# Four instead of three seven-product pairs in six value/gate panels of a retention layer, two in a row, and one factor moved from VectorE to ScalarE

## Chip, core and metric

One core of one Trainium2 chip runs the whole program. The metric is device time in microseconds (us) of that core. The kernel before takes 2566.95 us (median of three runs, 2566.91 to 2567.36).

## The reference

Two decoder layers over 256 positions of width 2048, in float32: a retention layer and a block-sparse attention layer, each followed by a gated MLP. Only the retention layer's input projection is touched here. Cut to that:

```
proj = h @ w_in                       # 256x2048 @ 2048x12288
q, k, v, g = split(proj)              # per head: q, k 256 wide; v, g 512 wide
inner = (q @ k.T) * decay             # chunked retention, 8 heads
o = inner @ v                         # (plus the state between chunks)
on = (o - mean(o)) * rsqrt(var(o) + eps)
y = silu(g) * on * gain               # then y @ w_out
```

## The kernel before

**Products in three parts.** Each float32 weight is used as a high part `wh` and a low part `wl` that add up to it, and so is each activation. A product takes three matmuls: high by high, high by low, low by high. ScalarE makes `wh` by a copy (line 221), and VectorE makes `wl` by a subtraction from the raw weight and `wh` (line 222). The weights stream from HBM into four buffers `raw` (1 MB each); `wh` and `wl` have four buffers each of 128x1024.

**Steps.** The program is one long list of steps, and each step consumes one buffer of `wh` and one of `wl`. `step` (through `issue_split`) emits the splits for the step three ahead, then the matmuls of the present one. Since there are four buffers, the split for a step can only be written when the matmuls of the step four before it are done. Tile's scheduler fixes the order of each engine's instructions when the program is built; each engine then runs its own list in that order, and semaphores order the engines against one another.

**A head.** Each of the eight retention heads (hd = 0 to 7 here; "two to seven" of the change are hd = 1 to 6) has three panels: q and k (four steps each, lines 344 and 347), then value and gate together (`panel_s`, line 390). The value/gate panel walks over the 2048 rows of the contraction in eight pairs of 128-row chunks. A pair is done in one of two ways.

- **Eight** (`A` in the sequence): two steps of 12 matmuls, eight products in all. It needs two splits of 128x1024.
- **Seven** (`S`): Winograd's form of Strassen's scheme, seven products, 21 matmuls, in four steps. Call them s1 (products 1 and 3, 6 matmuls), s2 (product 2, 3 matmuls), s3 (products 5 and 7, 6) and s4 (products 4 and 6, 6). The weights have to be combined first, in place in `raw`: after the split for s1, one 128x1024 addition (line 237) makes the blocks that s3 takes, and two 128x512 additions (lines 242 and 243) make those that s4 takes. s1, s3 and s4 have a 128x1024 split each, s2 one of 128x512. The activations' combinations ("forms") are made once, when `fresh` is set (line 410 on), and kept in four slots that lie in the not yet written end of `yT`.

`HEAD_SEQS` gives the order. Before: `AASASASA` with pairs 0, 2 and 4 as sevens in heads 0 to 6, and `AASAASAA` with two sevens in the last head. Between a head's second and third pair also come its scores (`ret_scores`: 12 small matmuls into `ps`, then on VectorE the product with the decay `pf`, on ScalarE its high part `ph`, on VectorE the low part `pl`).

**The end of a head.** In the next head's q panel, `ret_pv` multiplies by the values, takes mean and variance, has GpSimd compute the factor `rs` = (var + eps)^-0.5 (line 578), subtracts the mean and multiplies by silu(g) into `sg` (line 845), and multiplies `sg` by `rs` (line 847). Two steps later `ret_yT` transposes `sg` on TensorE (line 540) into `yT`.

Of the kernel before, what the change touches and what calls it, by code (L numbers as in the profile page):

```python
# [13 lines left out]
AF = mybir.ActivationFunctionType  # L14
ALU = mybir.AluOpType
# [4 lines left out]
S = 256  # L20
KC = D // P
RH, RDK, RDV = 8, 256, 512
# [46 lines left out]
def wide_seqs(first, second, n_slots=8):  # L69


    n = len(second)
    one = [(p, first.index(p) % n_slots if p in first else None, p in first) for p in range(n)]
    again = [(i % n_slots, p, False) for i, p in enumerate(first)][-n_slots:]
    again += [(again[i][0], p, True) for i, p in enumerate(first[:-n_slots])]
    again = again[: second.count("S")]
    others = [p for p in range(n) if p not in [q for _, q, _ in again]]
    two = []
    for c in second:
        slot, p, fresh = again.pop(0) if c == "S" else (None, others.pop(0), False)  # L80
        two.append((p, slot, fresh))
    return one, two


def head_seq(pairs, seq, fresh):

    again, others = list(enumerate(pairs)), [p for p in range(len(seq)) if p not in pairs]
    return [(*again.pop(0)[::-1], fresh) if c == "S" else (others.pop(0), None, False) for c in seq]


FFN_SEVENS = list(range(3, 22, 2))
FFN_SEQS = wide_seqs(FFN_SEVENS, "AAASASASASASASASASASAA")
RET_SEQS = wide_seqs([5, 7, 9, 11, 13, 15], "AAASASASASASAAAA")
HEAD_SEQS = [head_seq([0, 2, 4], "AASASASA", hd == 0) for hd in range(RH - 1)] + [head_seq([0, 2], "AASAASAA", False)]
MOB_SEQS = wide_seqs([3, 5, 7], "AAASAAAA")


def build(tc, a, out):
# [11 lines left out]
    act, dve, pe = nc.scalar, nc.vector, nc.tensor  # L110
# [171 lines left out]
    def emit(items):  # L282
        for unit, mms in items:
            units.append(unit)
            for hf, mm in enumerate(mms):
                emit_half(len(units) - 1, *(mm if isinstance(mm, tuple) else (hf, mm)))
# [225 lines left out]
    def aux_tile():  # L512

        if not wide[0]:
            return paux.tile([P, 512], F32, name="aux")
        if not spare:
            t = pacc.tile([P, 2, 512], F32, name="acc")
            spare.extend([t[:, 1, :], t[:, 0, :]])
        return spare.pop()

    def mm3(dst, lh, ll, rh, rl, start, stop):
        pe.matmul(dst, lhsT=lh, rhs=rh, start=start, stop=False)  # L522
        pe.matmul(dst, lhsT=lh, rhs=rl, start=False, stop=False)  # L523
        pe.matmul(dst, lhsT=ll, rhs=rh, start=False, stop=stop)  # L524
# [50 lines left out]
    def rstd(dst, src, mul, eps):  # L575
        v = sml.tile([P, 2], F32, name="v")
        dve.tensor_scalar(v, src, mul, eps, op0=ALU.mult, op1=ALU.add)
        nc.gpsimd.tensor_tensor(dst, v, mhalf, op=ALU.pow)
# [87 lines left out]
    def make_temps(pool, **tags):  # L666

        return lambda what: pool().tile([P, 512], F32, name=what, tag=tags[what])
# [96 lines left out]
    def ret_vg(then):  # L765

        m, sums, came = {}, {}, []

        def first():
            a, b = (ret["p1"].tile([P, 2, RDV], F32, name=n, tag=t) for n, t in (("sa", "qT"), ("sb", "kT")))  # L770
            sums.update({2: a[:, 0, :], 4: a[:, 1, :], 3: b[:, 0, :], 8: b[:, 1, :]})
            act.activation(sums[2], m[1], AF.Copy)
            dve.tensor_tensor(sums[3], m[6], sums[2], op=ALU.subtract)
            dve.tensor_tensor(sums[4], m[7], sums[3], op=ALU.add)

        def second():
            dve.tensor_tensor(sums[3], m[5], sums[3], op=ALU.add)
            dve.tensor_tensor(sums[8], m[5], sums[4], op=ALU.add)

        def tiles():  # L780
            ret["v"] = [ret["p1"].tile([P, 2, RDV], F32R, name=n) for n in ("vh", "vl")]
            ret["sg"] = ret["p1"].tile([P, 2, RDV], F32, name="sg")

        def done(b, acc):
            m[b] = acc
            if b == 6:
                after(0, first)
                after(1, second)
            if b not in (2, 3, 4, 8):
                return  # L790
            if not came:
                tiles()
            came.append(b)
            t, v = int(b in (4, 8)), sums[b]
            rt = r["r"][:, t : t + 1]
            dve.tensor_tensor(v, acc, v, op=ALU.subtract if b == 4 else ALU.add)
            if b in (3, 8):
                act.activation(ret["sg"][:, t, :], v, AF.Silu, scale=rt)
            else:
                vh, vl = (x[:, t, :] for x in ret["v"])  # L800
                act.activation(vh, v, AF.Copy, scale=rt)
                dve.scalar_tensor_tensor(vl, v, rt, vh.bitcast(F32), op0=ALU.mult, op1=ALU.subtract)
            if len(came) == 4:
                then()
        return done
# [20 lines left out]
    def ret_pv(hd):  # L826

        ph, pl = ret.pop(("p", hd))
        vh, vl = ret["v"]
        sg = ret["sg"]  # L830
        mv = sml.tile([P, 2, 2], F32, name="mv")
        po = [None, None]
        for t in range(2):
            po[t] = aux_tile()
            blocks = [(0, 0)] if t == 0 else [(P, 0), (S, 1)]
            for i, (c0, m) in enumerate(blocks):
                mm3(po[t], ph[:, c0 : c0 + P], pl[:, c0 : c0 + P], vh[:, m, :], vl[:, m, :],
                    i == 0, i == len(blocks) - 1)
            st = sml.tile([P, 6], F32, name="st")
            dve.bn_stats(st, po[t])  # L840
            dve.bn_aggr(mv[:, t, :], st)
        rs = sml.tile([P, 2], F32, name="rs")
        rstd(rs, mv[:, :, 1], 1.0, GN_EPS)
        for t in range(2):
            dve.scalar_tensor_tensor(sg[:, t, :], po[t], mv[:, t, 0:1], sg[:, t, :],
                                     op0=ALU.subtract, op1=ALU.mult)
            dve.tensor_scalar(sg[:, t, :], sg[:, t, :], rs[:, t : t + 1], None, op0=ALU.mult)

    def ret_yT(hd):
        y = ret["sg"]  # L850
# [11 lines left out]
    def ret_head(hd):  # L862
        def k_done(acc):
            ret_qk("k")(acc)
            after(4, lambda: ret_scores(hd))

        def vg_done():
            after(3, lambda: ret_pv(hd))
            after(5, lambda: ret_yT(hd))
            if hd == 0:  # L870
                after(6, lambda: bias_load())
                after(8, lambda: bias_table())

        q = panel_b(w_in, hd * RDK, xT_h, ret_qk("q"), before=ret_begin if hd == 0 else None)
        k = panel_b(w_in, D + hd * RDK, xT_h, k_done)
        if hd == 0:
            emit_pairs(q, k)
        else:
            emit(q + k)

        def unit(k0):
            vg = w_in[k0 * P : (k0 + 2) * P, 2 * D :].rearrange("(c p) (b n) -> p c b n", p=P, b=2)
            return vg[:, :, :, hd * RDV : (hd + 1) * RDV], 1024

        def slots(s):

            c = (28, 30, 24, 26)[s]
            return yT[0][:, c, :], yT[0][:, c + 1, :]

        emit(panel_s(unit, xT_h, HEAD_SEQS[hd], make_temps(lambda: ret["p1"], af="bs", ff="m1"), ret_vg(vg_done), slots))  # L890

# [296 lines left out]
```

## Time and profile before

| | before |
|---|---|
| median of three runs | 2566.95 us |
| profiled execution | 2566.55 us |
| its span, first to last instruction | 2564.8 us |
| TensorE (PE) busy | 2551.7 us, 99% |
| VectorE (DVE) busy | 2096.4 us, 82% |
| ScalarE (ACT) busy | 1445.2 us, 56% |
| mean granted TensorE clock | 0.999 of 2.4 GHz |
| bytes moved | 504.94 MB, mean 197 GB/s |

The 1.75 us between execution and span lie outside the instructions. Busy times of TensorE are sums of pipelined matmuls that overlap, so the pace of the matmuls is read from the distance of their starts, not from their durations. One retention head lasts 68.1 us.

### The profile page before, as it was taken

To read this page: it belongs to the slowest core of one execution; us is meant where nothing else is said; L and a number is where in the kernel's file an instruction comes from. 1 tells how busy PE (TensorE), PEld (TensorE's weight loads), DVE (VectorE), ACT (ScalarE), POOL (GpSimd) and SP (SyncE) were. 2 spreads that over 40 slices of the span, in tenths; PEclk is the share of its full clock that TensorE was granted. 3 is DMA by queue.
4 is the path that set the end of the run, shared out by engine and by line. 5 is a ranking of instruction groups with operands and counts; after the bars stand their busy time and mean duration, and the time that the engine had idled before them with its cause. 6 is when DMAs were issued, how large, how long until landed. Compare 5 with 4: busy or idle time off the path is not lost.

```text
span 2564.8 us, 34472 instructions
## 1 busy us (share of the span) xinstructions
PE 2551.7 (99%) x13280; PEld 2175.4 (85%) x13280; DVE 2096.4 (82%) x2740; ACT 1445.2 (56%) x1866; POOL 10.2 (0%) x24
## 2 busy tenths in 40 slices
PE   9999999999999999999999999999999999999998
PEld 8888888888888888888888888888888888888887
DVE  7888888898877777777898866668877777778998
ACT  6555555555555555555565655455655555555655
POOL 0000000000000000000000000000000000000000
PEclk9999999999999999999999999999999999999999
DMA  7765665555566566656665665555665656567654
GB/s 258 227 203 181 197 193 185 181 185 192 197 197 193 193 198 193 198 192 199 228 213 201 209 193 177 174 183 170 193 195 191 199 188 203 188 203 240 214 202 148
DMA packets 344532, 504.94 MB, mean 197 GB/s; under 512 B 9632, under 2 KB 260528, under 8 KB 344112
## 3 DMA queue, kind: packets, MB, share of 16 engines
q1 hardware_dynamic: 332720, 483.53, 57.5%
q10 hardware_dynamic: 11648, 19.22, 2.2%
q8 instruction: 104, 1.70, 0.3%
q14 instruction: 60, 0.49, 0.1%
HBM read 495.34 MB, written 10.51 MB: 197 GB/s over the span
## 4 chain that ended last, share of the span: by engine, by line
PE 97%; DVE 2%; ACT 1%; issue 0%; POOL 0%; POOLq 0%; ACTq 0%; DVEq 0%
PE acc L344 35%; PE aux L390 31%; PE acc L347 17%; PE acc L390 8%; PE acc L310 1%; PE acc L312 1%; PE acc L311 1%; DVE wl L222 1%; PE aux L540 1%; PE aux L523 0%; PE aux L524 0%; PE aux L522 0%; ACT wh L221 0%; PE aux L1110 0%; PE acc L523 0%
## 5 line engine op out<-in xcount | busy, mean ns | idle before, releaser
L221 ACT ACTIVATE wh<-raw 128x1024 fp32r<-128x1024 f32 (+2 forms) x1065 | 1083.8, 1028 | 1013.9 <-PE acc L344 459.0
L222 DVE TENSOR_TENSOR wl<-raw,wh 128x1024 fp32r<-128x1024 f32 (+2 forms) x1065 | 1240.9, 1182 | 407.6 <-ACT wh L221 398.9
L344 PE MATMUL acc<-hT,wh 128*128 128x512 f32 x3840 | 1208.9, 396 | 1.2 <-DVE hT L546 0.8
L347 PEld LDWEIGHTS acc<-hT,wl 128*128 128x128 f32 x3840 | 721.0, 188 | 170.3 <-DVE wl L222 0.6
L347 PE MATMUL acc<-hT,wl 128*128 128x256 f32 x3840 | 755.2, 278 | 0.2 <-DVE wl L222 0.2
L344 PEld LDWEIGHTS acc<-hT,wh 128*128 128x128 f32 x3840 | 586.2, 189 | 4.0 <-ACT wh L221 1.6
L390 PE MATMUL aux<-wh,actT 128*128 128x512 f32 x952 | 312.3, 389 | 0.0
L390 PE MATMUL aux<-wh,hT 128*128 128x512 f32 x854 | 285.1, 390 | 0.4 <-ACT wh L221 0.2
L390 PEld LDWEIGHTS aux<-wh,actT 128*128 128x128 f32 x952 | 178.7, 188 | 37.7 <-DVE h L620 0.5
L390 PEld LDWEIGHTS aux<-wh,hT 128*128 128x128 f32 x854 | 160.2, 188 | 35.1 <-ACT wh L221 1.6
L390 PE MATMUL aux<-wl,actT 128*128 128x512 f32 x476 | 185.2, 389 | 0.0
L390 PE MATMUL aux<-wl,hT 128*128 128x512 f32 x427 | 166.3, 390 | 0.0
L929 DVE SCALAR_TENSOR_TENSOR t<-u,cw,t 128x256 f32<-128x256 f32 x352 | 146.6, 478 | 0.0
L390 PE MATMUL aux<-wh,yT 128*128 128x512 f32 x426 | 141.8, 391 | 0.5 <-ACT yT L221 0.5
L390 PE MATMUL acc<-wh,hT 128*128 128x512 f32 x364 | 133.5, 390 | 0.0
L390 PEld LDWEIGHTS aux<-wl,actT 128*128 128x128 f32 x476 | 89.4, 188 | 18.2
L925 ACT ACTIVATE t<-u,cw 128x256 f32<-128x256 f32 x176 | 95.0, 586 | 0.1
L390 PEld LDWEIGHTS aux<-wh,yT 128*128 128x128 f32 x426 | 80.0, 188 | 17.6 <-ACT yT L221 0.9
L390 PEld LDWEIGHTS aux<-wl,hT 128*128 128x128 f32 x427 | 80.2, 188 | 16.7 <-DVE wl L222 0.3
L237 DVE TENSOR_TENSOR raw<-raw 128x1024 f32<-128x1024 f32 x76 | 92.5, 1217 | 0.0
L390 PE MATMUL aux<-wl,yT 128*128 128x512 f32 x213 | 83.0, 390 | 0.0
L745 DVE TENSOR_TENSOR bs<-acc,bs 128x512 f32<-128x512 f32 x120 | 81.9, 683 | 0.0
(208 smaller groups left out, 2024.2 us busy)
## 6 DMA issues: line engine op xcount, KB each, us to landing
raw<-in_ffn_w_up_dram SPq DMA_DIRECT2D x176, 1024.0 KB, 5.2
raw<-in_ffn_w_down_dram SPq DMA_DIRECT2D x88, 1024.0 KB, 5.5
raw<-in_ret_w_in_dram SPq DMA_DIRECT2D x133, 512.0 KB, 4.8
raw<-in_moba_w_qkv_dram SPq DMA_DIRECT2D x48, 1024.0 KB, 5.3
raw<-in_ret_w_out_dram SPq DMA_DIRECT2D x32, 1024.0 KB, 5.4
raw<-in_ret_w_in_dram SPq DMA_DIRECT2D x29, 1024.0 KB, 5.7
raw<-in_moba_w_out_dram SPq DMA_DIRECT2D x16, 1024.0 KB, 5.4
hT<-f ACTq DMA_DIRECT2D x22, 256.0 KB, 5.4
```

The source lines that it names most:

```text
L221: in_turn(act.activation(hi, src, AF.Copy))
L222: in_turn(dve.tensor_tensor(lo, src, hi.bitcast(F32), op=ALU.subtract))
L237: dve.tensor_tensor(b[:, 0:2, :], b[:, 0:4:3, :], b[:, 1:2, :].to_broadcast([P, 2, 512]), op=ALU.add)
L310: pe.matmul(acc, lhsT=xh, rhs=wh[:, c, :], start=(k == 0), stop=False)
L311: pe.matmul(acc, lhsT=xh, rhs=wl[:, c, :], start=False, stop=False)
L312: pe.matmul(acc, lhsT=xl, rhs=wh[:, c, :], start=False, stop=(k == nk - 1))
L344: pe.matmul(acc[:, b, :], lhsT=wh[:, c, b * P : (b + 1) * P], rhs=xt[:, k, :], start=(k == 0), stop=False)
L347: pe.matmul(acc[:, b, S:], lhsT=wl[:, c, b * P : (b + 1) * P], rhs=xt[:, k, :S], start=False, stop=(k == KC - 1))
L390: pe.matmul(acc[b], lhsT=xs, rhs=ws, start=(n == 1), stop=(n == uses[b]))
L745: dve.tensor_tensor(bs, acc[:, :, :S], bs, op=ALU.add)
L925: act.activation(t[:, i, :], u[:, i, 2:], AF.Identity, bias=c[:, 3, b : b + 1], scale=c[:, 2, b : b + 1])
L929: dve.scalar_tensor_tensor(t[:, i, :], u[:, i, tap : tap + S], c[:, tap, b : b + 1], t[:, i, :], op0=ALU.mult, op1=ALU.add)
```

## The change

Three things. In heads 1 to 6 the panel has four sevens, pairs 0, 2, 4 and 6, in the order `AASSASSA`: each time two sevens stand next to each other. Head 1 makes the forms for the new pair 6; heads 2 to 6 reuse them. Heads 0 and 7 keep their sequences. And in all eight heads the multiplication of `sg` by `rs` is an activation on ScalarE with a scale.

```
 def head_seq(pairs, seq, fresh):
-    again, others = list(enumerate(pairs)), [p for p in range(len(seq)) if p not in pairs]
-    return [(*again.pop(0)[::-1], fresh) if c == "S" else (others.pop(0), None, False) for c in seq]
+    again = [(p, i, p in fresh) for i, p in enumerate(pairs)]
+    others = [p for p in range(len(seq)) if p not in pairs]
+    return [again.pop(0) if c == "S" else (others.pop(0), None, False) for c in seq]
...
-HEAD_SEQS = [head_seq([0, 2, 4], "AASASASA", hd == 0) for hd in range(RH - 1)] + [head_seq([0, 2], "AASAASAA", False)]
+HEAD_SEQS = [head_seq([0, 2, 4], "AASASASA", [0, 2, 4])] + [head_seq([0, 2, 4, 6], "AASSASSA", [6] if hd == 1 else []) for hd in range(1, RH - 1)]
+HEAD_SEQS += [head_seq([0, 2], "AASAASAA", [])]
...
-            dve.tensor_scalar(sg[:, t, :], sg[:, t, :], rs[:, t : t + 1], None, op0=ALU.mult)
+            act.activation(sg[:, t, :], sg[:, t, :], AF.Copy, scale=rs[:, t : t + 1])
```

The change shifts all later lines by two: L222 of before is L224 of the changed kernel, L237 is L239, L820 is L822.

VectorE's list in the value/gate panel of head 4 (heads 2 to 6 have the same), from the scores to the third seven. `wl` 128x1024 and 128x512 are the splits, `raw` the additions, `pf` and `pl` the scores. Before:

```order
L222 TENSOR_TENSOR wl<-raw,wh 128x1024 x2
L820 TENSOR_TENSOR pf<-acc,dec 128x256
L821 TENSOR_TENSOR pf<-acc,dec 128x128
L823 TENSOR_TENSOR pl<-pf,ph 128x384
L222 TENSOR_TENSOR wl<-raw,wh 128x1024 x3
L222 TENSOR_TENSOR wl<-raw,wh 128x512
L237 TENSOR_TENSOR raw<-raw 128x1024
L242 TENSOR_TENSOR raw<-raw 128x512
L243 TENSOR_TENSOR raw<-raw 128x512
L222 TENSOR_TENSOR wl<-raw,wh 128x1024 x5
```

And the changed kernel, same place:

```order
L224 TENSOR_TENSOR wl<-raw,wh 128x1024 x2
L822 TENSOR_TENSOR pf<-acc,dec 128x256
L823 TENSOR_TENSOR pf<-acc,dec 128x128
L825 TENSOR_TENSOR pl<-pf,ph 128x384
L224 TENSOR_TENSOR wl<-raw,wh 128x1024
L224 TENSOR_TENSOR wl<-raw,wh 128x512
L239 TENSOR_TENSOR raw<-raw 128x1024
L244 TENSOR_TENSOR raw<-raw 128x512
L245 TENSOR_TENSOR raw<-raw 128x512
L224 TENSOR_TENSOR wl<-raw,wh 128x1024 x5
```

In both, the first row holds the splits of s3 and s4 of the first seven. Before, the next three 128x1024 splits are the two of an eight and s1 of the next seven; now the very next split is s1 of the second seven, and its additions follow with no eight between. The row of five is then s3, s4, the two of an eight, and s1 of the third seven; the fourth seven follows the third in the same way.

VectorE's list in head 1, where the forms are made, in the changed kernel: `af` and `ff` are the forms, `yT` 128x512 is the low part that goes into the slot. Before, the rows of `ff` and `yT` are absent, and in the second seven the addition of line 243 (L245 here) precedes the split of s3; the rest stands in the same order.

```order
L224 TENSOR_TENSOR wl<-raw,wh 128x512
L239 TENSOR_TENSOR raw<-raw 128x1024
L415 TENSOR_TENSOR ff<-af 128x256
L244 TENSOR_TENSOR raw<-raw 128x512
L416 TENSOR_TENSOR ff<-af,ff 128x128
L245 TENSOR_TENSOR raw<-raw 128x512
L417 TENSOR_TENSOR ff<-af,ff 128x128
L822 TENSOR_TENSOR pf<-acc,dec 128x256
L823 TENSOR_TENSOR pf<-acc,dec 128x128
L224 TENSOR_TENSOR wl<-raw,wh 128x1024
L825 TENSOR_TENSOR pl<-pf,ph 128x384
L224 TENSOR_TENSOR wl<-raw,wh 128x1024 x2
```

```order
L224 TENSOR_TENSOR wl<-raw,wh 128x512
L239 TENSOR_TENSOR raw<-raw 128x1024
L224 TENSOR_TENSOR yT<-ff,yT 128x512
L244 TENSOR_TENSOR raw<-raw 128x512
L224 TENSOR_TENSOR wl<-raw,wh 128x1024
L245 TENSOR_TENSOR raw<-raw 128x512
L224 TENSOR_TENSOR wl<-raw,wh 128x1024 x4
```

So three small rows of forms lie between the first seven's additions, and in the second seven the low part of the form stands ahead of `L244`, and `L245` behind the split of s3.

ScalarE's list in the q panel behind a head, in the changed kernel; `sg<-sg,rs` is the moved multiplication, `bs` the q panel's evacuation, `yT` the high parts behind the transposes. Before, the two rows of L849 are absent here, and one of the `wh` rows behind stands ahead of `bs`.

```order
L800 ACTIVATE sg<-sb,r 128x512 x2
L223 ACTIVATE wh<-raw 128x1024 x2
L849 ACTIVATE sg<-sg,rs 128x512
L746 ACTIVATE bs<-acc 128x512
L849 ACTIVATE sg<-sg,rs 128x512
L223 ACTIVATE wh<-raw 128x1024 x2
L545 ACTIVATE yT<-aux,laid 128x256 x4
```

SyncE's list, which issues the loads of the weights, is unchanged.

## Rows read from the trace of the kernel before

**Rows 1.** The page's busy times over the whole span (us, share, instructions), and the shares of the chain of waits that ended last.

```profile
PE 2551.7 (99%) x13280; PEld 2175.4 (85%) x13280; DVE 2096.4 (82%) x2740; ACT 1445.2 (56%) x1866; POOL 10.2 (0%) x24
...
PE 97%; DVE 2%; ACT 1%; issue 0%; POOL 0%; POOLq 0%; ACTq 0%; DVEq 0%
```

**Rows 2.** Busy time of each engine in three stretches: the program's first 10 us, head 4's value/gate panel with its scores, and one whole head from that panel's start. Columns: stretch, its length, busy us and number of instructions by engine, granted clock, DMA share, GB/s.

```profile
0.00:10.00 10.00, 8.04 (x43) 7.40 (x44) 2.62 (x8) 4.74 (x10) 0.30 (x5) 1.00 0.83 268
...
310.50:353.40 42.90, 42.90 (x197) 35.78 (x196) 37.13 (x44) 24.02 (x27) 0.00 (x0) 1.00 0.59 191
...
310.50:378.60 68.10, 68.10 (x342) 57.76 (x341) 59.61 (x77) 36.73 (x44) 0.69 (x1) 1.00 0.58 186
```

**Rows 3.** Timeline of TensorE in head 4. Columns: start, duration (of a merged group), engine, line, operation, output and inputs, shapes, count. 301.31 are the transposes of `sg` of the head before; 322.78 is the first matmul of the first seven, 327.60 that of the eight behind it, 333.04 that of the second seven; in it 335.08 and 335.31 are the first and second matmul of s3, 336.44 the first of s4; 337.80 is the eight behind it.

```profile
301.31 1.04 PE L540 MATMUL aux<-laid,sg 128*128 128x128 f32 x8
...
322.78 0.45 PE L390 MATMUL acc<-wh,hT 128*128 128x512 f32 x1
...
327.60 0.39 PE L390 MATMUL aux<-wh,hT 128*128 128x512 f32 x1
...
333.04 0.39 PE L390 MATMUL acc<-wh,hT 128*128 128x512 f32 x1
...
335.08 0.39 PE L390 MATMUL acc<-wh,yT 128*128 128x512 f32 x1
335.31 0.39 PE L390 MATMUL acc<-wl,yT 128*128 128x512 f32 x1
...
336.44 0.39 PE L390 MATMUL aux<-wh,hT 128*128 128x512 f32 x1
...
337.80 0.39 PE L390 MATMUL aux<-wh,hT 128*128 128x512 f32 x1
```

**Rows 4.** Timeline of ScalarE in head 4; in brackets the idle time before an instruction and what ended it.

```profile
324.58 0.53 ACT L822 ACTIVATE ph<-pf 128x384 fp32r<-128x384 f32 x1 [1.82 <-DVE pf L821]
325.01 3.49 ACT L221 ACTIVATE wh<-raw 128x1024 fp32r<-128x1024 f32 x4
331.43 1.06 ACT L221 ACTIVATE wh<-raw 128x1024 fp32r<-128x1024 f32 x1 [2.94 <-DVE raw L237]
333.29 1.06 ACT L221 ACTIVATE wh<-raw 128x1024 fp32r<-128x1024 f32 x1 [0.79 <-PE aux L390]
334.65 3.06 ACT L221 ACTIVATE wh<-raw 128x1024 fp32r<-128x1024 f32 x3 [0.30 <-PE aux L390]
```

**Rows 5.** Timeline of VectorE in head 4, columns as before. The group of four at 326.08 is three 128x1024 splits and the 128x512 one, which the view merges.

```profile
298.89 0.89 DVE L847 TENSOR_SCALAR sg<-sg,rs 128x512 f32<-128x512 f32 x2 [0.21 <-POOL rs L578]
...
322.79 1.23 DVE L222 TENSOR_TENSOR wl<-raw,wh 128x1024 fp32r<-128x1024 f32 x1 [1.36 <-ACT wh L221]
323.93 0.42 DVE L820 TENSOR_TENSOR pf<-acc,dec 128x256 f32<-128x256 f32 x1
...
325.13 0.56 DVE L823 TENSOR_TENSOR pl<-pf,ph 128x384 fp32r<-128x384 f32 x1 [0.59 <-ACT ph L822]
326.08 4.10 DVE L222 TENSOR_TENSOR wl<-raw,wh 128x1024 fp32r<-128x1024 f32 x4 [0.39 <-ACT wh L221]
330.10 1.22 DVE L237 TENSOR_TENSOR raw<-raw 128x1024 f32<-128x1024 f32 x1
331.35 0.69 DVE L242 TENSOR_TENSOR raw<-raw 128x512 f32<-128x512 f32 x1
332.08 0.69 DVE L243 TENSOR_TENSOR raw<-raw 128x512 f32<-128x512 f32 x1
332.69 1.22 DVE L222 TENSOR_TENSOR wl<-raw,wh 128x1024 fp32r<-128x1024 f32 x1
334.38 5.46 DVE L222 TENSOR_TENSOR wl<-raw,wh 128x1024 fp32r<-128x1024 f32 x5 [0.48 <-ACT wh L221]
```

**Rows 6.** Groups of instructions over the whole span (form, count | busy us, mean ns of one | idle before): a 128x512 copy with a scale on ScalarE, one without, and the multiplication that is moved.

```profile
L801 ACT ACTIVATE vh<-sa,r 128x512 fp32r<-128x512 f32 x16 | 11.5, 717 | 3.4 <-DVE sa L796 3.4
...
L744 ACT ACTIVATE bs<-acc 128x512 f32<-128x512 f32 x120 | 69.4, 579 | 0.5 <-DVE m L756 0.5
...
L847 DVE TENSOR_SCALAR sg<-sg,rs 128x512 f32<-128x512 f32 x16 | 7.1, 484 | 1.6 <-POOL rs L578 1.6
```

**Rows 7.** Timeline of VectorE in head 1, from the end of the k panel to the first seven's s4.

```profile
110.86 0.69 DVE L761 TENSOR_TENSOR kT<-m,kT 128x512 fp32r<-128x512 f32 x1 [0.70 <-ACT kT L760]
...
116.02 1.22 DVE L237 TENSOR_TENSOR raw<-raw 128x1024 f32<-128x1024 f32 x1
117.27 0.69 DVE L242 TENSOR_TENSOR raw<-raw 128x512 f32<-128x512 f32 x1
...
118.61 0.41 DVE L820 TENSOR_TENSOR pf<-acc,dec 128x256 f32<-128x256 f32 x1
...
119.14 1.21 DVE L222 TENSOR_TENSOR wl<-raw,wh 128x1024 fp32r<-128x1024 f32 x1
120.27 0.55 DVE L823 TENSOR_TENSOR pl<-pf,ph 128x384 fp32r<-128x384 f32 x1
```

**Rows 8.** Timeline of TensorE in head 1: the first matmul of the first seven, and the one in s3 that takes the low part.

```profile
118.36 0.45 PE L390 MATMUL acc<-wh,hT 128*128 128x512 f32 x1
...
120.68 0.39 PE L390 MATMUL acc<-wl,yT 128*128 128x512 f32 x1
```

**Rows 9.** Timeline of TensorE at the program's start: a matmul group behind a wait.

```profile
9.81 0.70 PE L344 MATMUL acc<-hT,wh 128*128 128x512 f32 x2 [0.84 <-DVE hT L546]
```

## The prediction

> **What bounds the kernel now.** I read the page's busy times and the chain of waits first. TensorE is busy 99% of the span, and 97% of the chain that ended last is TensorE's own work [rows 1]: nothing that another engine does faster shortens this program, but anything that reaches TensorE late lengthens it one for one. The table by stretches then shows the stage that is changed: in head 4's value/gate panel TensorE never idles (42.90 of 42.90 us), while VectorE is busy for 37.1 and ScalarE for 24.0; over a whole head VectorE has 59.6 of 68.1 [rows 2]. On average, then, VectorE has room. Whether it has it at the right moment is in the timelines of the three engines in that panel, which carry the forecast.
>
> The pace of a matmul is the distance of the starts. An eight has 24 matmuls from 327.60 to 333.04, 5.44 us; a seven has 21 from 333.04 to 337.80, 4.76 us [rows 3]. That is 0.227 us each, although one lasts 0.39.
>
> **The gain.** Six panels lose 3 matmuls each: 6 x 0.68 = 4.1 us. Durations would make it 6 x 3 x 0.39 = 7.0, but the starts count, as the matmuls overlap.
>
> **What VectorE gets.** A 128x1024 split takes 1.14 us up to the next instruction (322.79 to 323.93), the 128x512 one 0.60 (326.08 to 330.10 is three large and this one), and from the first addition to the split behind the three additions 2.59 (330.10 to 332.69) [rows 5]. A seven is therefore 3 x 1.14 + 0.60 + 2.59 = 6.61 us of VectorE in 4.76 us of TensorE, an eight 2.28 in 5.44. A seven between eights borrows from them. Two in a row cannot: the buffers let VectorE run no more than four steps ahead, that is, one seven. So the question is how late the second seven's s3 is, which stands behind all three additions.
>
> **First two sevens, heads 2 to 6.** Up to the first seven's s4 nothing is moved. The first seven starts at 322.78; what follows it, now the second seven, starts at 327.60, and the second matmul of s3, the first that takes `wl`, is due 335.31 - 333.04 = 2.27 later, at 329.87 [rows 3]. On VectorE the s4 split (322.79), `pf` and `pl` come first, and the next split has to wait for its `wh`, which ScalarE makes behind `ph`, from 325.01 to 326.07 [rows 4]; so it starts at 326.08 [rows 5]. This slot passes from the eight to the second seven's s1. From there: 1.14 + 0.60 to the first addition (327.82), 2.59 to the split of s3 (330.41), 1.22 for it: 331.63. That is 1.76 us after 329.87, 1.8 with a handover of 0.03 (`wh` done at 333.29 + 1.06, split at 334.38 [rows 4, 5]). The s4 split then ends at 330.41 + 1.14 + 1.22 = 332.77 and is needed six matmuls after the resumption, at 333.03: no second stall, and none in the eight behind.
>
> **Third and fourth seven, heads 1 to 6.** Between the two couples stands an eight, so the third seven is like today's lone one. Measured from its start: `wh` of its s4 waits for the eight's last matmuls (333.29, that is +0.25), and the s4 split starts at +1.34; the next `wh` waits for the buffer that s1 holds, until +1.61 (334.65), and is done at +2.67 [rows 3 to 5]. The fourth seven's s1 split thus starts at +2.70, its small one at 3.84, the additions at 4.44, the s3 split at 7.03, done at 8.25. Due is 4.76 + 2.27 = 7.03. Late by 1.25 with the handover.
>
> **Head 1.** Here VectorE is later today: the s3 split of the first seven starts at 119.14, ends at 120.35 and is due at 120.68 [rows 7, 8]. The forms come on top. `af` (a 128x512 addition, 0.69 as line 242) falls into the 0.70 us wait before `kT`, and costs nothing; without this cover it would cost 0.6. The three `ff` between the additions cost about 0.6: the first (0.41 by `pf`'s row of the same shape) mostly fills the gap between lines 237 and 242, which waits for a result [rows 7]. So s3 is late by 0.3, and s4, behind `pl` and its `wh`, by 0.3 more. In the second seven the small split into `yT` (0.60) stands ahead of line 242 and line 243 behind the s3 split: s3 late by 1.85 as above, but now s4's `wh` can start only after line 243: 0.7 + 1.06 + 1.22 behind the s3 split, where six matmuls cover 1.36: 1.65. Together 4.1. Bounds: 1.8, if head 1 were like the others, and 4.7.
>
> **The factor on ScalarE.** VectorE loses 0.89 us per head in the q panel [rows 5], ScalarE gets two 128x512 copies with a scale, 0.72 each by the nearest row, at least 0.58 by the copy without one [rows 6]. `rs` is there at 298.89, when VectorE starts on it today. Then ScalarE's list has copy, `bs`, copy: 298.9 + 0.62 + 0.50 + 0.72 = 300.75 at their pace of about 0.1 below duration. The transposes start at 301.31 [rows 3]: covered by 0.55 us. The `wh` behind is about 2 us later than today, but its step is three steps (8 us) ahead. I take 0; without that cover it would be the lateness times eight heads, at most 0.3 x 8 = 2.4. Nothing is gained either: the 0.89 us are freed long before the panel, where the s4 split waits for `wh` and that for TensorE's eight [rows 4, 5], so an earlier VectorE only waits longer.
>
> **The sum.** -4.1 + 5 x 1.8 + 6 x 1.25 + 4.1 = +16.5 us. The profiled execution's 2566.55 becomes 2583.05, and the median of before is 0.4 above its profiled execution: **2583.4 us**, 0.64% slower. A measurement of this kernel tells about 0.2% (5.1 us) from no change.
>
> Own range of this case: low with 1.25 for the first couple too (if scores cost nothing), 1.0 for the second (if its s1 split followed s4's at +2.48) and 1.25 in head 1: -4.1 + 6.25 + 6.0 + 1.25 = +9.4, 2576. High with 0.1 of handover at each of some 15 stalls, 4.7 in head 1 and 2.4 for the transposes: +21, 2588.
>
> **Rivals.**
>
> *The additions are hidden; no stall (the other side).* Then only the gain stays: 2562.9, within 0.2%. For it speaks the average, 59.6 of 68.1 us. It would need the s3 splits of second sevens 1.25 to 1.8 us earlier, that is, two more `wh`/`wl` buffers, or the additions ahead of the first seven's s4. It decides where the second seven's s1 split starts more than 1.8 us earlier than at 326.08; ScalarE's row at 325.01 speaks against it. Chance 0.05. More than 4.1 us cannot be gained, so faster by over 0.2% needs something unseen: 0.02.
>
> *Only the second couple stalls.* If the VectorE time freed in the q panel let `pf`, `pl` and the next `wh` come earlier, the first couple would be hidden, head 1's too: 7.5 - 4.1 = +3.4, 2570.4, within 0.2%. Against it: `pf` waits for TensorE's scores, which end at 322.78. Chance 0.04.
>
> *TensorE's clock falls behind the new stalls.* All through the profile the clock stands at the upper level of 2.4 GHz. At the start TensorE idled for 0.84 us and went on with 0.70 us for two matmuls [rows 9], with 1.00 granted over these 10 us [rows 2]. At the lower level a matmul would take 0.453 instead of 0.227. If one step of 2.7 us behind each of some 13 stalls ran so, that is +35 on top of 16.5, 2618; a whole panel in each of six heads would be +240. Chance 0.02, as the stalls are 1 to 2 us in 40 us of work. The Trainium skill has a rule against changes of this kind (TensorE: Matmul & The Clock Gate, "A second HAM failure mode: psum-queue depth-cycling"): a kernel whose TensorE idled briefly and often between groups of matmuls had the clock swing between the levels. By that rule the time would be 2618 or more; the trace agrees with it in nothing so far, as the idle above left the clock alone.
>
> *Stalls at about half their size*, from an order effect that I miss: +6, 2573. Chance 0.03.
>
> The likeliest has 0.84. The range 2576 to 2589 is its own, and leaves out the rivals and a little of its tails. Faster 0.02; within 0.2% 0.09; slower 0.89.
>
> **What would show it.** In the changed profile TensorE should wait at line 392 (390 of before) for `wl` about 13 times, 1.2 to 1.9 us each, some 20 us in all, in heads 1 to 6 alone, always in a second seven's s3 (in head 1 at s4 too); heads 1 to 6 should last some 70.5 us instead of 68.1, head 1 72 to 73; VectorE's idle time in those panels should nearly vanish ahead of the second sevens; the transposes of `sg` should not wait. I am wrong if the longest wait on `wl` is below 0.5 us, if the waits stand in the eights or the q panels, or if the granted clock falls.

## The result

The changed kernel takes 2585.5 us (median of four runs, 2584.6 to 2585.8) against 2567.15 of before beside it: a ratio of 1.0071, 95% interval 1.0058 to 1.0084. That is 18.4 us slower; 16.5 were forecast. The profiled execution took 2585.4 us; its span is 2583.6.

The page of the changed kernel, busy times and the shares of the chain that ended last, answers to [rows 1]:

```profile
PE 2555.9 (99%) x13262; PEld 2171.1 (84%) x13262; DVE 2117.6 (82%) x2759; ACT 1465.0 (57%) x1895; POOL 10.2 (0%) x24
...
PE 93%; DVE 4%; ACT 2%; issue 1%; POOL 0%; ACTq 0%; POOLq 0%; DVEq 0%
```

From the table of what TensorE waited for, the rows of the value/gate panel (us in total, times, longest; one wait of 0.2 us on `wh` stands in the kernel before too):

```profile
PE aux L392 <- ACT wh L223: 11.2, 14, 1.0
PE acc L392 <- ACT wh L223: 2.9, 6, 0.6
...
PE acc L392 <- DVE wl L224: 0.8, 1, 0.8
```

The first line of busy times hardly differs from before. The chain does: TensorE's own share fell from 97 to 93%, VectorE's and ScalarE's rose from 3 to 6%. That is where the time went, and the waits at line 392, the value/gate panel, name the place.

Windows of the changed kernel, columns as in [rows 2]: 70.5 us, nearly one of the heads 2 to 6 as they now are (70.9), and 2.1 us around the two waits of its first couple.

```profile
299.00:369.50 70.50, 68.15 (x337) 56.68 (x336) 62.68 (x80) 38.98 (x49) 0.69 (x1) 1.00 0.53 178
...
340.50:342.60 2.10, 1.02 (x3) 0.66 (x4) 2.03 (x3) 1.71 (x3) 0.00 (x0) 1.00 0.02 4
```

In the 70.5 us TensorE is busy for 68.15, where before it was never idle; in the short window it stands still for half the time, while VectorE works for 2.03 of 2.10 us. The granted clock is 1.00 in both.

TensorE's timeline in head 4, for [rows 3]: the transposes of `sg`, the second seven from its start to the eight behind it, then the fourth.

```profile
311.65 1.03 PE L542 MATMUL aux<-laid,sg 128*128 128x128 f32 x8
...
337.98 0.39 PE L392 MATMUL acc<-wh,hT 128*128 128x512 f32 x1
...
339.79 0.39 PE L392 MATMUL aux<-wh,hT 128*128 128x512 f32 x1
340.63 0.49 PE L392 MATMUL acc<-wh,yT 128*128 128x512 f32 x1 [0.45 <-ACT wh L223]
342.08 0.50 PE L392 MATMUL aux<-wh,hT 128*128 128x512 f32 x1 [0.96 <-ACT wh L223]
342.42 0.40 PE L392 MATMUL acc<-wl,yT 128*128 128x512 f32 x1
342.66 0.63 PE L392 MATMUL acc<-wh,yT 128*128 128x512 f32 x2
...
344.75 0.39 PE L392 MATMUL aux<-wh,hT 128*128 128x512 f32 x1
...
354.95 0.39 PE L392 MATMUL acc<-wh,hT 128*128 128x512 f32 x1
...
357.09 0.50 PE L392 MATMUL acc<-wh,yT 128*128 128x512 f32 x1
358.53 0.50 PE L392 MATMUL aux<-wh,hT 128*128 128x512 f32 x1 [0.94 <-ACT wh L223]
358.87 0.40 PE L392 MATMUL acc<-wl,yT 128*128 128x512 f32 x1
...
361.20 0.39 PE L392 MATMUL aux<-wh,hT 128*128 128x512 f32 x1
```

A seven without a stall takes 4.76 us. The second one lasts 344.75 - 337.98 = 6.77, 2.01 too long; the fourth 361.20 - 354.95 = 6.25, 1.49 too long. 2.01 + 1.49 - 0.68 = 2.82 us per head. One row stands in a place that the prediction had not seen: the matmul at 342.08 (`aux<-wh,hT`) is the first of s4, and it stands ahead of s3's first `wl` matmul (342.42) in TensorE's list. So the wait is booked on `wh` of s4, not on `wl` of s3.

VectorE's timeline in the same couple, for [rows 5]:

```profile
336.43 1.83 DVE L224 TENSOR_TENSOR wl<-raw,wh 128x1024 fp32r<-128x1024 f32 x2 [0.39 <-ACT wh L223]
338.18 1.22 DVE L239 TENSOR_TENSOR raw<-raw 128x1024 f32<-128x1024 f32 x1
339.43 0.69 DVE L244 TENSOR_TENSOR raw<-raw 128x512 f32<-128x512 f32 x1
340.16 0.69 DVE L245 TENSOR_TENSOR raw<-raw 128x512 f32<-128x512 f32 x1
340.77 5.92 DVE L224 TENSOR_TENSOR wl<-raw,wh 128x1024 fp32r<-128x1024 f32 x5
```

And ScalarE's, for [rows 4]:

```profile
339.51 1.06 ACT L223 ACTIVATE wh<-raw 128x1024 fp32r<-128x1024 f32 x1 [2.59 <-PE aux L392]
340.97 4.61 ACT L223 ACTIVATE wh<-raw 128x1024 fp32r<-128x1024 f32 x5 [0.39 <-DVE raw L245]
```

From 336.43 VectorE works without a gap: two splits, three additions, five splits. The s3 split starts at 340.77 and ends 1.22 later, at 341.99. ScalarE's cast for s4 waits for the last addition and ends at 340.97 + 1.06 = 342.03. Both `wl` of s3 and `wh` of s4 are thus there at 342.0, and TensorE resumes at 342.08. The cast for s3 at 339.51 is booked on a matmul of TensorE that ended about then, but the addition of line 239 ended at 338.18 + 1.22 = 339.40, 0.11 ahead of it, and by the same 0.11 the cast followed that addition before (330.10 + 1.22 to 331.43 [rows 4, 5]): it waits for the addition.

The moved factor, ScalarE's timeline in head 4's q panel:

```profile
309.31 0.73 ACT L849 ACTIVATE sg<-sg,rs 128x512 f32<-128x512 f32 x1 [4.20 <-POOL rs L580]
309.95 0.58 ACT L746 ACTIVATE bs<-acc 128x512 f32<-128x512 f32 x1
310.43 0.71 ACT L849 ACTIVATE sg<-sg,rs 128x512 f32<-128x512 f32 x1
311.04 1.99 ACT L223 ACTIVATE wh<-raw 128x1024 fp32r<-128x1024 f32 x2
```

The second half of `sg` is done at 311.14, the transposes start at 311.65 and wait for nothing: covered by 0.51 us, where 0.55 was worked out. One instruction lasts 0.718 us, as the nearest row [rows 6] said.

### The profile page after: what moved, and what is told of

Read it like the earlier page. It is cut to its first block, busy times and chain, and to the rows that moved or that the text cites. A ratio compares the mean times of both kernels' runs of the same rounds, so it can differ in the third digit from the quotient of the medians.

```text
span 2583.6 us, 34474 instructions
## 1 busy us (share of the span) xinstructions
PE 2555.9 (99%) x13262; PEld 2171.1 (84%) x13262; DVE 2117.6 (82%) x2759; ACT 1465.0 (57%) x1895; POOL 10.2 (0%) x24
## 4 chain that ended last, share of the span: by engine, by line
PE 93%; DVE 4%; ACT 2%; issue 1%; POOL 0%; ACTq 0%; POOLq 0%; DVEq 0%
PE acc L346 34%; PE aux L392 28%; PE acc L349 17%; PE acc L392 7%; DVE wl L224 2%; ACT wh L223 1%; PE acc L312 1%; PE acc L314 1%; PE acc L313 1%; DVE raw L239 1%; PE aux L542 1%; PE aux L525 0%; PE aux L526 0%; PE aux L524 0%; DVE raw L244 0%
## 5 line engine op out<-in xcount | busy, mean ns | idle before, releaser
L224 DVE TENSOR_TENSOR wl<-raw,wh 128x1024 fp32r<-128x1024 f32 (+2 forms) x1077 | 1251.0, 1181 | 399.7 <-ACT wh L223 390.6
L392 PE MATMUL aux<-wh,hT 128*128 128x512 f32 x782 | 265.6, 392 | 11.3 <-ACT wh L223 11.2
L392 PEld LDWEIGHTS aux<-wh,hT 128*128 128x128 f32 x782 | 146.6, 188 | 47.2 <-ACT wh L223 16.9
L392 PE MATMUL aux<-wl,hT 128*128 128x512 f32 x391 | 152.4, 390 | 0.0
L392 PEld LDWEIGHTS aux<-wl,actT 128*128 128x128 f32 x476 | 89.4, 188 | 18.4
L239 DVE TENSOR_TENSOR raw<-raw 128x1024 f32<-128x1024 f32 x82 | 100.0, 1219 | 0.0
L392 PEld LDWEIGHTS aux<-wl,hT 128*128 128x128 f32 x391 | 73.4, 188 | 15.6 <-DVE wl L224 0.4
```

What stands on the lines that cost most here:

```text
L224: in_turn(dve.tensor_tensor(lo, src, hi.bitcast(F32), op=ALU.subtract))
L239: dve.tensor_tensor(b[:, 0:2, :], b[:, 0:4:3, :], b[:, 1:2, :].to_broadcast([P, 2, 512]), op=ALU.add)
L392: pe.matmul(acc[b], lhsT=xs, rhs=ws, start=(n == 1), stop=(n == uses[b]))
```

## Where the time stands in each kernel

All runs below are read with one measure: the start of the first score matmul of each head (in the changed kernel 331.79 in head 4, 402.75 in head 5). "Head 1" is from that of head 1 to that of head 2, "heads 2 to 6" the mean of the next five distances, "rest" from that of head 7 to the end of the span.

| kernel | median, us | head 1 | heads 2 to 6 | rest |
|---|---|---|---|---|
| before | 2566.9 to 2567.2 | 68.23 | 68.10 | 2039.0 |
| changed | 2585.5 | 72.57 | 70.92 | 2039.0 |
| factor alone | 2566.95 | 68.24 | 68.10 | 2039.2 |
| sevens alone | 2585.1 | 72.55 | 70.88 | 2039.0 |
| three sevens, two in a row | 2579.8 | 71.92 | 70.09 | 2038.9 |
| half an eight between | 2572.7 | 71.01 | 68.70 | 2038.9 |
| two additions out | 2577.8 | 70.59 | 69.87 | 2038.9 |
| three additions out | 2563.4 | 68.11 | 67.43 | 2038.9 |
| matmuls in written order | 2608.4 | 85.69 | 70.85 | 2053.4 |
| fifth buffer | 2583.1 | 69.87 | 69.08 | 2047.7 |
| its control, four buffers | 2597.9 | 73.15 | 71.59 | 2047.8 |
| small split on GpSimd | 2595.0 | 75.40 | 72.35 | 2038.9 |
| half an eight, and that | 2582.2 | 72.13 | 70.40 | 2039.0 |

## Experiments: which part

**The factor alone.** The kernel before with only the factor on ScalarE.

```
-            dve.tensor_scalar(sg[:, t, :], sg[:, t, :], rs[:, t : t + 1], None, op0=ALU.mult)
+            act.activation(sg[:, t, :], sg[:, t, :], AF.Copy, scale=rs[:, t : t + 1])
```

> The kernel before with only the factor moved to ScalarE. Theory (the whole cost is the wait of a second seven for its additions and splits): no change, 2566 to 2568.5. Rival (ScalarE's longer list in the q panel delays `bs`, `wh` or the transposes): 2 to 18 us slower, with TensorE waiting at the transposes of `sg` or at line 344.

Measured 2566.95 (2566.33 to 2567.09) against 2566.97, ratio 1.0000 (0.9991 to 1.0009). The factor's move costs and gives nothing.

**The sevens alone.** The factor back on VectorE.

```
-            act.activation(sg[:, t, :], sg[:, t, :], AF.Copy, scale=rs[:, t : t + 1])
+            dve.tensor_scalar(sg[:, t, :], sg[:, t, :], rs[:, t : t + 1], None, op0=ALU.mult)
```

> The changed kernel with the factor back on VectorE. Theory: as slow as the changed kernel, 2584 to 2587, with the same two waits in every head. Rival (the factor carries a share of the cost): clearly faster than 2584.

2585.1 us, ratio 1.0071 (1.0057 to 1.0085), and the same waits on `wh` (11.2 us in 14 and 2.9 in 6): the whole cost is in the sevens.

**Two in a row without a fourth.** Heads 1 to 6 keep three sevens, but the first two stand next to each other; the factor stays on VectorE.

```
...
-head_seq([0, 2, 4, 6], "AASSASSA", [6] if hd == 1 else [])
+head_seq([0, 2, 4], "AASSASAA", [])
...
```

> As before three sevens (pairs 0, 2, 4) in heads 1 to 6, but in the order AASSASAA, so two of them side by side; factor on VectorE; no matmul is saved. Theory (adjacency costs): about 2.0 us for the couple in each of six heads, +12, 2577 to 2581, and the third seven, behind an eight, waits for nothing. Rival (the cost comes from the number of sevens, that is, from VectorE's work per head, which is unchanged here): 2567.

2579.8 us, ratio 1.0050 (1.0035 to 1.0065), within the expected. Heads 2 to 6 last 1.99 us longer than before, which is the first couple's stall by itself (2.01 in the changed kernel), with the same two waits:

```profile
337.77 0.50 PE L392 MATMUL acc<-wh,yT 128*128 128x512 f32 x1 [0.47 <-ACT wh L223]
339.22 0.50 PE L392 MATMUL aux<-wh,hT 128*128 128x512 f32 x1 [0.95 <-ACT wh L223]
```

So neighbourhood is the price, not the number of sevens.

Head 1 lasts 3.69 us longer than before, 1.70 more than that. It makes no forms here; what differs is the clock. Behind the two waits of its couple (0.57 and 0.95 us) TensorE was granted 0.50 of its clock, the lower level of 1.2 GHz, for 3.41 us, and its matmuls started 0.43 us apart instead of 0.227. TensorE's timeline in head 1:

```profile
125.90 0.49 PE L392 MATMUL acc<-wh,yT 128*128 128x512 f32 x1 [0.57 <-ACT wh L223]
127.35 0.50 PE L392 MATMUL aux<-wh,hT 128*128 128x512 f32 x1 [0.95 <-ACT wh L223]
...
129.16 0.63 PE L392 MATMUL acc<-wh,yT 128*128 128x512 f32 x1
129.59 0.63 PE L392 MATMUL aux<-wl,hT 128*128 128x512 f32 x1
```

And that stretch as a window, columns as in [rows 2]:

```profile
127.94:131.35 3.41, 3.41 (x10) 2.67 (x9) 3.31 (x4) 2.32 (x3) 0.00 (x0) 0.50 0.81 250
```

Half the speed for 3.41 us costs 1.7. Heads 2 to 6 have nearly the same waits (0.47 and 0.95 us), and their clock stays at 1.00.

**Half an eight between any two sevens.** Four sevens per head, but the two steps of an eight are taken apart, one behind each seven; with it the additions behind the last seven's end come one step sooner.

```
...
-                after(1, second)
+                after(0, second)
...
+            turns = [(0, 2), (1, 2), (2, 4), (4, 1), (3, 4), (4, 1), (5, 4), (7, 1), (6, 4), (7, 1)]
...
```

> The changed kernel, still four sevens in heads 1 to 6, but one step (half) of an eight between any two of them: steps in the order A A S, half A, S, half A, S, half A, S, half A; the additions behind the last seven's end come one step sooner. Theory (adjacency): a half eight gives TensorE 2.72 us of work for 1.14 us of VectorE, so the second seven gains 1.6 us of lead; about 0.1 to 0.4 us of wait is left in each of three places, 0.7 per head, which the saved 0.68 pay: 2564 to 2569, within 0.2% of before. Rival (four sevens are too much work for VectorE wherever they stand): 2578 or more.

2572.7 us, ratio 1.0023 (1.0013 to 1.0032): most of the cost is gone, yet some 4 us more than expected stay. VectorE's timeline in head 4 shows why:

```profile
333.12 1.22 DVE L239 TENSOR_TENSOR raw<-raw 128x1024 f32<-128x1024 f32 x1
...
335.71 5.39 DVE L224 TENSOR_TENSOR wl<-raw,wh 128x1024 fp32r<-128x1024 f32 x5
341.02 1.22 DVE L239 TENSOR_TENSOR raw<-raw 128x1024 f32<-128x1024 f32 x1
...
343.60 5.39 DVE L224 TENSOR_TENSOR wl<-raw,wh 128x1024 fp32r<-128x1024 f32 x5
```

VectorE doesn't pause in this stretch, and from one seven's additions to the next are 7.90 us, while TensorE's 21 + 12 matmuls want 33 x 0.227 = 7.48. Most of the missing 0.42 shows in TensorE's timeline at s3 of the second, third and fourth seven, as a wait for `wl` of some 0.23 and a slow step behind it (0.46 and 0.34 where 0.227 is the pace):

```profile
336.52 0.39 PE L392 MATMUL acc<-wh,yT 128*128 128x512 f32 x1
336.98 0.50 PE L392 MATMUL acc<-wl,yT 128*128 128x512 f32 x1
337.32 0.63 PE L392 MATMUL acc<-wh,yT 128*128 128x512 f32 x2
```

Heads 2 to 6 last 0.60 us more than before instead of 0.68 less, and head 1, with its forms, 2.78 more: 5 x 0.60 + 2.78 = 5.8. Here, by this timeline, the balance of VectorE's work against TensorE's is the limit, over a seven and half an eight; no run that lightens it without a side effect was made (see the small split on GpSimd below).

## Experiments: which link of the chain

**Two additions out.** The second seven of each couple leaves out the two additions of lines 244 and 245, so its last products take plain blocks.

```
+        def split_b21_alone(raw, wh, wl):
+            b = blocks(raw)
+            split_to(wh[:, :512], wl[:, :512], b[:, 2, :])
...
```

> The changed kernel; the second seven of each couple leaves out the two additions of 128x512 on its combined blocks (the two of L244 and L245), so that its last products take plain blocks. Theory (the chain to the last two steps counts, first addition, ScalarE's cast, VectorE's split; the two additions only delay what stands behind them): the split of step three still waits for the cast behind its own addition, and is done some 0.2 to 0.35 us earlier; the fourth step's cast is not behind an addition any more: 3 to 6 us less than the changed kernel, 2579.5 to 2582.5 us. Rival (VectorE's total time in the couple is the price): the two additions' 1.3 us come back whole in some 12 couples: about 2569 us.

2577.8 us, ratio 1.0042 (1.0027 to 1.0057). Between the two: 1.05 us per head come back, 0.53 per couple, where the one theory had 0.2 to 0.35 and the other 1.3. The total work on VectorE is not the price (1.3 us less of it gave 0.53); but the cast of s4's `wh`, which no longer waits for line 245, came 0.5 us earlier, and TensorE's list puts that matmul first: the couple's second wait fell from 0.96 to 0.44. I had left that out.

**Three additions out.** As well the addition of line 239; the seven still multiplies seven times.

```
+        def split_b11_b22_alone(raw, wh, wl):
+            split_to(blocks(wh), blocks(wl), blocks(raw)[:, 0:4:3, :])
...
```

> The changed kernel; the second seven of each couple leaves out all three additions on its blocks, so that it splits plain blocks as an eight does, but still multiplies seven times. Theory (the additions and what waits behind them are late, not the seven's missing product): the stalls of heads 2 to 6 go to 0.3 us or less per couple; what stays is the gain of 4.1 us and some of head 1's: 2563 to 2568 us. Rival (a product less per seven leaves too little time for the splits themselves): 2575 us or more.

2563.4 us, ratio 0.9986 (0.9977 to 0.9996), as expected: the panel has no wait that the kernel before hasn't, and heads 2 to 6 last 67.43 us, 0.67 less than before. That is the gain of 0.68 per head as it was worked out, and it shows that the additions in the second seven, with what queues behind them, are all of the stall in these heads. On VectorE's timeline in head 4 eight splits then follow each other without a pause, the second seven's four, the eight's two and the next seven's first two:

```profile
325.10 8.30 DVE L224 TENSOR_TENSOR wl<-raw,wh 128x1024 fp32r<-128x1024 f32 x8 [0.39 <-ACT wh L223]
```

**TensorE's list in written order.** If s4's first matmul did not stand ahead of s3's `wl`, would the wait be shorter?

```
-                pe.matmul(acc[b], lhsT=xs, rhs=ws, start=(n == 1), stop=(n == uses[b]))
+                tc.keep_in_program_order(pe.matmul(acc[b], lhsT=xs, rhs=ws, start=(n == 1), stop=(n == uses[b])))
```

> The changed kernel with all matmuls of these panels kept in the order in which they are written, so that the first matmul of step four doesn't stand ahead of step three's `wl` matmul in TensorE's list. Nothing is left out. Theory (in head 4 that matmul waits 0.96 us for step four's `wh` with a ready one behind it): each couple in heads 2 to 6 gets 0.2 us shorter, 2 to 3 us in all: 2582 to 2584 us. Rival (the reordering fills a wait that would be there anyway): within 1 us of 2585.

2608.4 us, ratio 1.0159 (1.0144 to 1.0174), outside both expectations, but the total answers another question: the order was kept in every panel of this kind, and now other matmuls stand behind late ones (up to 2.9 us for `kT`, 2.8 for `yT`), in head 1 and in the rest. Within or behind such waits the granted clock was 0.50 in three stretches, 13.65 us in all, which is some 6 us of the loss; none of them lies in heads 2 to 6. Heads 2 to 6 answer it: 70.85 against 70.92. The rival is right. Timeline of TensorE in head 4:

```profile
349.39 0.49 PE L392 MATMUL acc<-wh,yT 128*128 128x512 f32 x1 [0.47 <-ACT wh L223]
350.81 0.50 PE L392 MATMUL acc<-wl,yT 128*128 128x512 f32 x1 [0.92 <-DVE wl L224]
351.14 0.63 PE L392 MATMUL acc<-wh,yT 128*128 128x512 f32 x2
```

The same two waits, 0.47 and 0.92, and now the second one is on `wl`, as predicted. The hoisted matmul only changes the name in the wait.

## Experiments: how it could be hidden

**A fifth buffer.** One of the prediction's rivals said that the additions could be hidden with more lead. It named two more buffers; this run adds one. In the retention heads `wh` and `wl` get a fifth buffer and the splits run one step further ahead. To make room, the decay of head 0 serves all heads and the taps of layer 0 both layers.

```
+        fifth = 8 <= i < state["heads"] and i % 5 == 4
+        wh = ret["p1"].tile([P, 1024], F32R, name="whx") if fifth else whi.tile([P, 1024], F32R, name="wh")
+        wl = ret["p1"].tile([P, 1024], F32R, name="wlx") if fifth else wlo.tile([P, 1024], F32R, name="wl")
...
-        ahead = 0 if i == 0 else 1 if i < 3 else 2 if i < 8 else LOOKAHEAD
+        ahead = 0 if i == 0 else 1 if i < 3 else 2 if i < 8 else LOOKAHEAD + (i + 4 < state["heads"])
```

> The changed kernel with a fifth buffer for `wh` and `wl` in the retention heads and the weights prepared one step further ahead there. To make room in SBUF the decay of head 0 is used for all heads, and the convolution taps of layer 0 for both layers. Theory (the preparation of the second seven of a couple is late because it can only begin when one of four buffers comes free): one step more of lead takes most of the stall away, the first couple's 2.0 us falls to about 0.5 and the second's 1.5 to about 0.1, so some 11 couples give back 1.4 us each: 2567 to 2572 us. Rival (VectorE has more work in a couple than the seven products last, wherever it begins): the stall only moves, 2580 us or more.

2583.1 us, ratio 1.0063 (1.0046 to 1.0080). By the total the rival would be right. But the rest, where nothing else differs, lasts 2047.7 instead of 2039.0 us, and that is not the buffer's doing if the room made for it did it. Hence a control:

**The same room, four buffers.** Against the kernel with the fifth buffer, `fifth` and both its uses are gone, and the lead is the old one.

```
...
-        ahead = 0 if i == 0 else 1 if i < 3 else 2 if i < 8 else LOOKAHEAD + (i + 4 < state["heads"])
+        ahead = 0 if i == 0 else 1 if i < 3 else 2 if i < 8 else LOOKAHEAD
```

> The control of the run with a fifth buffer: the changed kernel with the same room made in SBUF (the decay of head 0 for all heads, the taps of layer 0 for both layers), but with four buffers and the old lead. With the fifth buffer the heads lost 7.5 us against before instead of 18.4, but the rest of the program, where nothing is changed and nothing waits, lasted 8.7 us longer. Theory A (the smaller tables put other tiles at other addresses, and that alone slows the rest): the heads as in the changed kernel and 8 to 9 us lost behind them: 2592 to 2596 us. Theory B (it is the fifth buffer itself): no loss behind the heads, 2585 us within 2.

2597.9 us, ratio 1.0120 (1.0106 to 1.0134), 2 us above the expected, and the rest again 2047.8: theory A in the rest, where the loss comes with the smaller tables and without the fifth buffer. But theory A had the heads as in the changed kernel, and heads 2 to 6 last 0.67 us longer, at no more waiting (11.2 and 2.1 us against 11.2 and 2.9): the smaller tables slow the heads too. Against this control the fifth buffer gives back 14.8 us, where the theory had some 11 x 1.4 = 15.4, and 2.51 per head in heads 2 to 6. In the kernel with the fifth buffer TensorE waits in this panel for (the line is one later there):

```profile
PE aux L393 <- ACT wh L224: 2.6, 8, 0.5
```

and in its control for:

```profile
PE aux L392 <- ACT wh L223: 11.2, 14, 1.0
PE acc L392 <- ACT wh L223: 2.1, 6, 0.5
```

So the lead of four buffers is what makes two sevens in a row late; one step more hides 2.5 of some 3.5 us per head.

**The small split on GpSimd.** It is busy for 10.2 us in the whole program, and the 128x512 split of s2 is 0.60 us ahead of the additions.

```
...
+        nc.gpsimd.tensor_tensor(wl[:, :512], b[:, 2, :], wh[:, :512].bitcast(F32), op=ALU.subtract)
...
```

> The changed kernel with the small split (128x512, 0.60 us on VectorE) of each seven's step two on GpSimd in heads 1 to 6. Nothing is left out. Theory (what stands ahead of step three's additions on VectorE is late one for one): the additions of the second seven start 0.6 us earlier, and each of 12 couples gives back about 0.6 us: 2577 to 2580 us. Rival (GpSimd takes longer for it than step one's matmuls cover, 1.36 us, or slows VectorE beside it): 2584 us or more.

> The order with half an eight between any two sevens, with the small split of step two on GpSimd in heads 1 to 6. Nothing is left out. Without the GpSimd part a seven and half an eight gave VectorE 6.61 + 1.14 = 7.75 us of work in 4.76 + 2.72 = 7.48 us of TensorE, 0.27 too much, and each later seven waited some 0.23 us, 0.34 with the slow restart. Theory (the balance decides): with 7.15 in 7.48 the small waits go, 1.28 us in each of heads 2 to 6, and some of head 1's 3.4: 2564 to 2567 us. Rival (GpSimd is late or in the way): 2572 us or more.

2595.0 us, ratio 1.0107 (1.0093 to 1.0121), and 2582.2 us, ratio 1.0059 (1.0045 to 1.0073): the rival in both, each some 9.5 us slower than without it. In the profile of the first, some 3.4 of them are the clock's: behind waits of 1.66 and 1.02 us in head 1, and of 0.94 and 1.35 in head 6, TensorE was granted 0.50, twice for 3.41 us (windows, columns as in [rows 2]). The second has no such stretch.

```profile
130.61:134.02 3.41, 3.41 (x10) 2.64 (x9) 3.41 (x4) 2.09 (x3) 0.00 (x0) 0.50 0.53 144
492.43:495.84 3.41, 3.41 (x10) 2.63 (x9) 3.41 (x4) 2.00 (x2) 0.00 (x0) 0.50 0.59 160
```

What is left, some 1.0 us in each of the six heads, has another cause. GpSimd's timeline in the first of the two, in head 4:

```profile
341.65 1.81 POOL L250 TENSOR_TENSOR wl<-raw,wh 128x512 fp32r<-128x512 f32 x1 [7.75 <-ACT wh L249]
```

VectorE's at the same time:

```profile
342.35 2.20 DVE L239 TENSOR_TENSOR raw<-raw 128x1024 f32<-128x1024 f32 x1
```

Beside GpSimd's instruction VectorE's addition lasts 2.20 us instead of 1.22: 0.98 is lost where 0.60 was to be gained. It ends 1.09 us after GpSimd does (341.65 + 1.81 = 343.46; 342.35 + 2.20 = 344.55), nearly its whole length. The Trainium skill (SBUF — State Buffer, "Who interferes with whom") says that a VectorE instruction with two inputs in SBUF contends with a GpSimd instruction that reads SBUF, and that the port pair they share is an exclusive lock; this row agrees.

No kernel here that does the whole work beats the one before. At most 4.1 us, 0.16%, were to be had, and the closest with four sevens is 0.23% slower.

## Why the prediction was right

- **The gain.** 0.68 us per head was forecast from the starts of the matmuls; the kernel without the second sevens' additions shows 0.67.
- **VectorE's chain.** The first addition of the second seven was forecast 5.04 us behind the first seven's start, the s3 split 7.63. Measured from 333.12: 338.18 (5.06) and 340.77 (7.65).
- **First couple, heads 2 to 6.** 1.8 forecast, 2.01 measured. The split of s3 was due, by the forecast's own distance, at 333.12 + 7.09 = 340.21, and ended at 341.99: 1.78 late, as forecast (1.76). What was too small is the handover: 0.03 was taken; TensorE resumes 0.09 later, and the second matmul behind the wait comes after 0.34 (342.08 to 342.42) instead of 0.227. Those two are 0.17 of the 0.21.
- **Third and fourth seven.** 1.25 forecast, 1.49 measured; the same resumption is in it (358.53 to 358.87).
- **Head 1.** 4.1 forecast for its first couple. Its gaps over 0.227 add up to 3.5: 0.56 in the first seven (0.6 forecast), 1.86 at the second's s3 (1.85), and 1.10 at its s4 (1.65), where TensorE's list puts a matmul that is ready into the wait:

```profile
130.00 0.50 PE L392 MATMUL aux<-wh,hT 128*128 128x512 f32 x1 [0.34 <-ACT wh L223]
130.34 0.40 PE L392 MATMUL acc<-wh,yT 128*128 128x512 f32 x1
130.95 0.73 PE L392 MATMUL aux<-wh,hT 128*128 128x512 f32 x2 [0.22 <-ACT wh L223]
```

- **The sum.** Heads 2 to 6 gave 5 x 2.82 = 14.1 (11.9 forecast), head 1 4.3 (4.7): 18.4 in place of 16.5. The miss is the term "handover", some 0.2 at each couple; head 1, forecast 0.4 too high, hides a little of it, by luck.
- **What would show it.** Right in place and in the length of heads 2 to 6 (70.9, forecast 70.5) and head 1 (72.6, forecast 72 to 73). Wrong in the size of a wait: the table of waits counts from the modelled end of the matmul before, and has some 14.7 us with none above 1.0, where 20 us and 1.2 to 1.9 each were expected; measured by the starts, 5 x 3.50 and head 1's 3.52 + 1.49 make 22.5 us late. And wrong in the name. The waits are on `wh`, one for s3 and one for s4, since I had read VectorE's list of the changed kernel but not TensorE's. A reader who had looked for a wait on `wl` alone would have found one, of 0.8 us, in head 1: the prediction's own limit of 0.5 us on that name was passed by this one wait.
- **The clock.** It stayed at the upper level, 0.999 on average and 1.00 in the 2.1 us window with two waits. (As before, only the last microseconds, with no matmul left, have the lower one; "all through the profile" in the prediction overlooks them.) The rule of the Trainium skill weighed in the prediction (TensorE: Matmul & The Clock Gate, "A second HAM failure mode: psum-queue depth-cycling") did not come into play in this profile. But this rival was nearer than its chance of 0.02: with two sevens in a row and much the same waits, 0.57 and 0.95 us, the clock did fall in one head of the run with three sevens, and it fell again in the runs in written order and with the split on GpSimd. The forecast gives no reason why the changed kernel was spared; that is luck, though one fall would have left the time within the range. The price was less than the forecast had: 1.7 us a time, and matmuls 0.43 us apart instead of 0.453.

## What to carry to other kernels

An engine that has an eighth of its time free on average, as VectorE in these heads, can still be the bound where work comes in lumps: with N buffers it can only borrow N steps, so two lumpy items next to each other must fit together, not only on average. Work this out by walking the late engine's list from the last wait that holds it, with pitches and not durations; add to each new wait the slow resumption of the waiting engine. And check the waiting engine's list too: the scheduler may put another matmul first, which changes what the wait is called and little else. Look at the granted clock of every run before its total is read: one fall of 3.41 us is 1.7 us of the time.

## What the runs showed of the hardware

- **A wait costs more than it lasts.** The matmul behind a wait lasts 0.49 to 0.50 us instead of 0.39, and the next one follows 0.33 to 0.35 us later instead of 0.227: 0.11 us at each wait, alike at 337.32 (half an eight between), behind a wait of 0.23, and at 342.42 (changed kernel), behind one of 1.2.
- **The clock behind short waits.** In three of the twelve other profiles TensorE was granted 0.50 for 3.41 us or 6.83: behind waits of 0.57 and 0.95 us (three sevens), 1.66 and 1.02, 0.94 and 1.35 (small split on GpSimd), and within or behind waits of 1.36 and 0.54, 2.91, and 2.33 (written order). The changed kernel's waits of 0.45 and 0.96 us, in five heads, brought no fall. What decides is open: waits of about the same length stand on both sides.
- **GpSimd beside VectorE.** A 128x512 subtraction takes GpSimd 1.59 to 2.23 us beside VectorE's work, and a VectorE addition that meets it goes from 1.22 to 2.20.
- **Room in SBUF and pace.** With the two smaller tables the unchanged rest of the program lasted 8.7 us longer (0.43%), in both kernels that had them, at a mean granted clock of 0.999 and with no new wait in the trace. Smaller tables presumably put the tiles allotted behind them at other addresses; whether the address is what counts, and why, stays open: no run moved a tile alone.
